# A two-block transformer step on one core: low halves of the weights by an accumulating DMA in place of a subtraction

## The chip, the cores and the metric

One core of a Trainium2 chip runs the whole program in one launch. The metric is the device time of one execution in microseconds (us).

## The reference

Two blocks work on 512 tokens of width 1024. The first block mixes with two kinds of attention (8 heads each of 64), attends to 256 memory rows (4 heads of 256) and has a gated FFN with a short convolution. The second block has a gating mixer over 128-token blocks, an MLP, a latent attention (8 heads) and a second MLP. Cut to its products:

```python
proj = rmsnorm(x) @ w_in                        # 1024 x 3080
x = x + concat(fox_attention, stick_breaking) @ w_out
x = x + softmax(q @ k.T / 16) @ v @ w_mo        # q from w_mq, k and v of the memory from w_mkv
u = causal_conv(rmsnorm(x) @ w_up)              # 1024 x 5632
x = x + (silu(gate) * val) @ w_down             # 2816 x 1024
h = h + (u * (W_s v + b)) @ a_w_out             # u, v = gelu(hn @ a_w_in)
h = h + square(relu(rmsnorm(h) @ w1)) @ w2      # 1024 x 4096 x 1024, twice
h = h + mla(hn) @ b_w_o
```

## The kernel before

Every fp32 product is made of three matmuls of a format with fewer bits: each operand is split into a high half (a cast to `F32R`) and a low half (what the cast lost), and `mm3` (L196) adds high by high, high by low and low by high. Activations are split once and stay. Weights are streamed: `weights` (L169) makes one unit of k rows of tiles by n columns, most often 128 partitions x 1024 numbers (512 KB), in these steps.

- SyncE loads the unit from HBM into `st`, tile `wst` (L176). The pool `p_wst` has 2 buffers (L118).
- ScalarE casts it to the high half, `wh` (L181). The pool `p_w` has 4 buffers for `wh` and 4 for `wl` (L119).
- VectorE or GpSimd subtracts: `wl = wst - wh` (L182). Which of them is named by a letter of `self.low`: "d" is VectorE, "p" is GpSimd. In the mixers the letters are taken from `LOW`, in the latent attention from `LATENT_LOW`; elsewhere all are "d".

A unit whose rows are scaled by gains (`gain`, 16 units for the latent projections) is made by `split` (L160) instead. With `apart` the very first unit goes in two halves.

The products are `tform` (L203: the weights are the stationary side, one unit is one chunk of 128 outputs), `tokens` (L212: the activations are stationary) and `down` and `last_down` (L274, L978: second products, unit by unit over the inner dimension, with the activation chunk split at L271 beside each unit). The stages run in order: `begin`, `mixers`, `memory`, `ffn`, `gmlp`, `mlp(0)`, `mla`, `mlp(1)` (L483 to L491). In the mixers and the latent attention, tables of due times (`FILL`, `LATENT_FILL` and others) weave the heads' work with units of later products. Then a scheduler orders the instructions of each engine by a simulated timeline; each engine takes its own in that order, one after the other.

GpSimd's other work is masks (L688), scaling of probabilities (L259), sums of squares (L349), additions at boundaries (L396), powers (L321), the FFN's gate product (L902) and the gating product (L1103). ScalarE's evacuations that the text speaks of are L954 (MLP, `square`) and L892 (FFN).

Of the kernel before, what the change touches and what calls it, by code (L numbers as in the profile page):

```python
# [12 lines left out]
F32 = mybir.dt.float32  # L13
# [4 lines left out]
ALU = mybir.AluOpType  # L18
# [42 lines left out]
def weave(*lanes):  # L61

    heap = [(times[0], i, 0) for i, (times, _) in enumerate(lanes)]
    heapq.heapify(heap)
    while heap:
        t, i, k = heapq.heappop(heap)
        times, gen = lanes[i]
        if next(gen, None) is not None:
            k += 1
            heapq.heappush(heap, (times[min(k, len(times) - 1)], i, k))  # L70


def even(t0, t1, n):
    return [t0 + (i + 0.5) * (t1 - t0) / n for i in range(n)]


def filling(gens, plan, t0):

    times, parts = [], []
    for i, (name, n, t1) in enumerate(plan):  # L80
        times += even(t0, t1, n)
        more = any(name == later[0] for later in plan[i + 1:])
        parts.append(itertools.islice(gens[name], n) if more else gens[name])
        t0 = t1
    return times, itertools.chain(*parts)


def run(gen):
    for _ in gen:
        pass  # L90
# [2 lines left out]
FILL = [['qk1', 16, 0.8], ['qk3', 16, 2.082], ['qk2', 12, 2.247], ['qk2', 4, 3.296], ['v', 32, 5.5], ['qk4', 16, 7.129], ['qk5', 16, 8.229], ['qk6', 10, 8.354], ['mk', 12, 8.992], ['qk6', 1, 9.307], ['mk', 8, 10.003], ['mk', 6, 10.525], ['qk6', 5, 10.752], ['mk', 8, 11.39], ['qk7', 16, 12.667], ['mv', 32, 15.302], ['out', 32, 16.79]]  # L93
FOX_SCALE = 'pppd'
LATENT_SCALE = 'dpad'
LOW = 'ppppppdppppp'
LATENT_LOW = 'ddpppppppppp'
NORM_FOX = 12.316
SCORES = [-0.68, 0.106]
MIX_OUT = 1.347  # L100
# [7 lines left out]
class Kernel:  # L108
# [60 lines left out]
    def weights(self, src, shape, gain=None, apart=False):  # L169

        k, n = shape
        low = next(self.low)
        st = self.p_wst.tile([P, k, n], F32, tag="wst", name="wst")
        parts = [slice(j, j + 1) for j in range(k)] if apart else [slice(0, k)]
        for j in parts:
            self.nc.sync.dma_start(st[:, j], src[:, j])  # L176
        h = self.p_w.tile([P, k, n], F32R, tag="wh", name="wh")
        l = self.p_w.tile([P, k, n], F32R, tag="wl", name="wl")
        if gain is None:
            for j in parts:  # L180
                self.nc.scalar.copy(h[:, j], st[:, j])  # L181
                self.engines[low].tensor_sub(l[:, j], st[:, j], h[:, j].bitcast(F32))  # L182
        else:
            for j, g in enumerate(gain):
                self.split(h[:, j], l[:, j], st[:, j], scale=g)
        return h, l
# [292 lines left out]
    def run(self):  # L479
        a, nc = self.a, self.nc  # L480
        self.steps, self.later, self.waiting, self.turn = 0, [], [], 6
        self.engines, self.low = {"d": nc.vector, "p": nc.gpsimd}, itertools.repeat("d")
        self.begin()  # L483
        self.mixers()
        self.memory()
        self.ffn()
        self.gmlp()
        self.rope_tables()
        self.mlp(0)
        self.mla()  # L490
        self.mlp(1)  # L491

    def begin(self):
# [16 lines left out]
        for b in range(NB):  # L510
            self.ingest(b, xs[b], g, xT, self.x)
            block = next(values)
            if b == 0:
                run(itertools.islice(block, 7))
            nc.vector.tensor_copy(col[:, b:b + 1], self.block_rstd(xs[b]))
            run(block)
# [197 lines left out]
    def mixers(self):  # L714
        a, nc = self.a, self.nc
        self.qk, self.rows = {}, {}
        cd = self.forget()
        self.sb_scale = self.scaled_cols(0.125)
        run(self.qk_pair(0))
        self.low = itertools.cycle(LOW)  # L720
        mixed = [self.s8([P, 4, T]) for _ in range(2)]
        accs = [self.t2("acc") for _ in range(2)]
        v_sb = []
        parts, fox_part = {}, []

        def stats(kind, bank):
            return self.spread(self.rstd_from(self.mean_sq(accs[kind], 512, bank=bank), NB), bank)

        def split_mixed(kind, row=None):

            parts[kind] = self.s8([P, 4, T], F32R), self.s8([P, 4, T], F32R)
            for pr in range(4):
                m = mixed[kind][:, pr]
                g = self.g[("fox", "sb")[kind]][:, pr:pr + 1]
                if row is not None:
                    nc.vector.scalar_tensor_tensor(m, m, g, row, op0=ALU.mult, op1=ALU.mult)
                self.split(*(t[:, pr] for t in parts[kind]), m, scale=g if row is None else None)

        def normed_fox():
            row = stats(0, "f")  # L740
            yield 1
            split_mixed(0, row)
            yield 1

        def fox_out():

            fox_part.extend(self.s8([P, 4, T]) for _ in range(2))

            def evac(m, ps):
                nc.scalar.copy(fox_part[m // 4][:, m % 4], ps)  # L750

            yield from self.down(lambda k: tuple(t[:, k] for t in parts[0]), a["w_out"][0, 0:512], 4, evac,
                                 [(range(3), range(4)), (range(3, 6), range(4)), (range(6, 8), range(4))], bank="f")

        def values_sb():
            v_sb.extend(self.s8([P, NB, 4, 2, 64], F32R) for _ in range(2))
            for block in self.vproj(v_sb, 2560):
                yield from block

        gens = {"mk": self.memory_keys(), "mv": self.memory_values(), "v": values_sb(), "out": fox_out()}  # L760
        gens.update({f"qk{pr}": self.qk_pair(pr) for pr in range(1, 8)})
        lanes = [filling(gens, FILL, -0.4), ([NORM_FOX, NORM_FOX + 0.3], normed_fox())]
        for hd in range(16):
            kind = hd // 8
            v = (self.v_fox, v_sb)[kind]
            head = self.fox_head(hd, cd) if kind == 0 else self.sb_head(hd - 8)
            lanes.append((even(hd + SCORES[0], hd + SCORES[1], 4), head))
            lanes.append(([hd + MIX_OUT + t for t in ATTEND], self.mix_head(hd, v, mixed[kind], accs[kind])))
        weave(*lanes)
        self.low = itertools.repeat("d")  # L770
        self.x = [self.s8([P, 4, T]) for _ in range(2)]
        for h in range(2):
            nc.scalar.dma_start(self.x[h].rearrange("p k t -> p (k t)"), self.x_dram[h])
        split_mixed(1)
        for m in range(8):
            nc.gpsimd.tensor_add(self.xc(m), self.xc(m), fox_part[m // 4][:, m % 4])
        out = self.down(lambda k: tuple(t[:, k] for t in parts[1]), a["w_out"][0, 512:1024], 4,
                        self.boundary(self.g["xattn"], rows=False, scale=lambda: row),
                        [(range(3), range(3)), (range(3, 7), range(3)), (range(3), [3]), (range(3, 7), [3]), ([7], range(4))], 1)
        run(itertools.islice(out, 21))  # L780
        row = stats(1, "o")
        run(out)
# [387 lines left out]
    def mla(self):  # L1170
        a, nc, n = self.a, self.nc, self.norm
# [53 lines left out]
        def values(pr):  # L1225

            u = self.w_rows(wkv, 0, 2, 512 * pr, 512)
            v = self.s8([P, NB, 2, 256], F32R)
            kv[pr] = u, v
            for b2 in range(2):  # L1230
                ps = self.ps("f")
                for b in range(2):
                    cols = slice((2 * b2 + b) * P, (2 * b2 + b + 1) * P)
                    out = ps[:, 256 * b:256 * b + 256].rearrange("p (h n) -> p h n", n=P)
                    for k in range(2):
                        xh, xl = ckv.at(k)
                        vw = tuple(t[:, k].rearrange("p (h n) -> p h n", n=256)[:, :, 128:256] for t in u)
                        self.mm3(out, (xh[:, cols], xl[:, cols]), vw, k == 0, k == 1)
                    yield 1
                s = slice(2 * b2, 2 * b2 + 2)  # L1240
                self.split(v[:, s, 0], v[:, s, 1], ps.rearrange("p (b n) -> p b n", b=2))
# [30 lines left out]

        self.low = itertools.cycle(LATENT_LOW)
        run(values(0))
# [85 lines left out]
            lanes.append((even(hd + LATENT_SCORES[0], hd + LATENT_SCORES[1], 4), scores(hd)))  # L1360
            lanes.append(([hd + LATENT_OUT + t for t in LATENT_ATTEND], outputs(hd)))
        weave(*lanes)
        self.low = itertools.repeat("d")
        run(out)


# [21 lines left out]
```

## Time and profile before

| | us |
|---|---|
| median of 2 runs | 2012.53 (2012.41 to 2012.64) |
| profiled execution | 2014.74 |
| its span, first to last instruction | 2013.0 |
| TensorE busy | 1962.5 |
| VectorE busy | 1149.5 |
| ScalarE busy | 881.7 |
| GpSimd busy | 385.4 |

Busy times come from one profiled execution; the span leaves out 1.7 us around the first and the last instruction. Matmuls overlap in their pipeline, so a full TensorE row means that one started as soon as the one before allowed it. DMA-issuing instructions are not counted as busy.

### The profile page before, as it was taken

The page shows a single profiled execution, that of the slowest core. Times are in us where ns is not written, and L with a number is a line of the kernel's source. Part 1 is how long each engine was busy: PE and PEld are TensorE (multiplying, and loading weights), DVE is VectorE, ACT ScalarE, POOL GpSimd, SP SyncE. Part 2 cuts the span into 40 slices and gives each one's busy share as a digit, 9 for nine tenths or more (in the row PEclk, how much of TensorE's full clock was granted, in tenths as well). Part 3 has the DMA queues.
Part 4 walks back from the last instruction along what each step waited for, and adds up shares of the span by engine and source line. Part 5 has one row for each costly group of instructions (what it writes and reads, how often), then busy time and mean ns, then how long its engine had stood idle before and what let it go on. Part 6 is the DMA issues. An engine that isn't in the chain of part 4 may idle for free.

```text
span 2013.0 us, 24501 instructions
## 1 busy us (share of the span) xinstructions
PE 1962.5 (97%) x9199; PEld 1633.6 (81%) x9199; DVE 1149.5 (57%) x1968; ACT 881.7 (44%) x1531; POOL 385.4 (19%) x316
## 2 busy tenths in 40 slices
PE   8998899999999999999999999999999999999998
PEld 7786777788888888888888888888898878888887
DVE  6778886547766533756875733333477774333334
ACT  6667564435443332545344432223356644322223
POOL 2675774202111100401220100000032320000000
PEclk9998999999999999999999999999999999999999
DMA  6322334213333322332223333232232123332232
GB/s 182 105 85 74 95 96 135 59 61 105 105 94 95 103 96 94 95 94 84 82 79 104 108 97 94 96 103 95 72 89 61 54 60 112 95 98 91 95 99 80
DMA packets 216391, 187.24 MB, mean 93 GB/s; under 512 B 12321, under 2 KB 189001, under 8 KB 215761
## 3 DMA queue, kind: packets, MB, share of 16 engines
q1 hardware_dynamic: 213953, 178.32, 29.7%
q10 hardware_dynamic: 2320, 7.36, 1.0%
q8 instruction: 72, 1.18, 0.2%
q14 instruction: 46, 0.38, 0.1%
HBM read 181.44 MB, written 4.21 MB: 92 GB/s over the span
## 4 chain that ended last, share of the span: by engine, by line
PE 81%; DVE 9%; ACT 3%; issue 3%; DMA 3%; POOL 2%; SPq 0%; POOLq 0%; ACTq 0%; DVEq 0%
PE ps_f L199 13%; PE ps_f L201 12%; PE ps_f L200 12%; PE ps_s L200 6%; PE ps_s L199 6%; PE ps_s L201 6%; PE ps_t L199 6%; PE ps_t L200 6%; PE ps_t L201 6%; PE ps_o L200 2%; PE ps_o L199 2%; PE ps_o L201 2%; DMA wst<-in_w_in 1%; DVE ex L690 1%; DVE wl L182 1%
## 5 line engine op out<-in xcount | busy, mean ns | idle before, releaser
L181 ACT CAST wh<-wst 128x1024 fp32r<-128x1024 f32 (+4 forms) x352 | 344.4, 979 | 648.8 <-PE ps_f L200 296.9
L182 DVE TENSOR_TENSOR wl<-wst,wh 128x1024 fp32r<-128x1024 f32 (+4 forms) x296 | 352.4, 1191 | 291.9 <-ACT wh L181 283.1
L201 PE MATMUL ps_f<-s,wl 128*128 128x512 f32 (+1 forms) x912 | 351.8, 387 | 3.8 <-DVE wl L182 3.8
L200 PE MATMUL ps_f<-s,wh 128*128 128x512 f32 (+1 forms) x912 | 352.6, 387 | 1.9 <-DVE s L167 1.8
L199 PE MATMUL ps_f<-s,wh 128*128 128x512 f32 (+1 forms) x912 | 349.2, 390 | 2.7 <-DVE f L805 1.5
L201 PEld LDWEIGHTS ps_f<-s,wl 128*128 128x128 f32 x912 | 173.1, 190 | 37.7 <-DVE wl L182 4.6
L199 PEld LDWEIGHTS ps_f<-s,wh 128*128 128x128 f32 x912 | 173.3, 190 | 36.0 <-DVE f L805 1.7
L200 PEld LDWEIGHTS ps_f<-s,wh 128*128 128x128 f32 x912 | 172.8, 190 | 34.2 <-DVE s L167 3.0
L349 POOL TENSOR_TENSOR acc<-acc,sq 128x512 f32<-128x512 f32 x46 | 75.5, 1648 | 633.8 <-ACT sq L348 632.9
L163 ACT CAST ch<-s 128x512 fp32r<-128x512 f32 (+1 forms) x166 | 77.5, 495 | 152.7 <-PE ps_s L200 100.2
L182 POOL TENSOR_TENSOR wl<-wst,wh 128x1024 fp32r<-128x1024 f32 (+3 forms) x56 | 123.7, 2212 | 98.6 <-ACT wh L181 98.6
L164 DVE TENSOR_TENSOR cl<-s,ch 128x512 fp32r<-128x512 f32 (+1 forms) x166 | 85.8, 535 | 87.5 <-ACT ch L163 87.5
L321 POOL TENSOR_TENSOR sm<-sm,m_half 128x1 f32<-128x1 f32 (+1 forms) x31 | 26.6, 859 | 495.1 <-DVE sm L338 351.9
L199 PE MATMUL ps_s<-s,wh 128*128 128x512 f32 x280 | 109.5, 392 | 0.4 <-ACT pp L849 0.4
L200 PE MATMUL ps_s<-s,wh 128*128 128x512 f32 x280 | 109.2, 390 | 0.0
L201 PE MATMUL ps_s<-s,wl 128*128 128x512 f32 x280 | 109.0, 390 | 0.0
L199 PE MATMUL ps_t<-s,wh 128*128 128x512 f32 x272 | 105.9, 390 | 0.0
L200 PE MATMUL ps_t<-s,wh 128*128 128x512 f32 x272 | 105.9, 389 | 0.0
L201 PE MATMUL ps_t<-s,wl 128*128 128x512 f32 x272 | 105.1, 389 | 0.0
L200 PE MATMUL ps_f<-cl,wh 128*128 128x512 f32 x210 | 82.1, 391 | 0.0
L199 PE MATMUL ps_f<-wh,s 128*128 128x512 f32 (+2 forms) x208 | 77.2, 376 | 4.8 <-ACT s L163 3.3
L201 PE MATMUL ps_f<-ch,wl 128*128 128x512 f32 x210 | 81.8, 389 | 0.0
(460 smaller groups left out, 4122.2 us busy)
## 6 DMA issues: line engine op xcount, KB each, us to landing
wst<-in_mlp_w SPq DMA_DIRECT2D x128, 512.0 KB
wst<-in_w_up SPq DMA_DIRECT2D x44, 512.0 KB
wst<-in_a_w_in SPq DMA_DIRECT2D x32, 512.0 KB
wst<-in_w_in SPq DMA_DIRECT2D x23, 512.0 KB
wst<-in_w_down SPq DMA_DIRECT2D x22, 512.0 KB
wst<-in_w_mkv SPq DMA_DIRECT2D x16, 512.0 KB
wst<-in_a_w_out SPq DMA_DIRECT2D x16, 320.0 KB
wst<-in_w_mq SPq DMA_DIRECT2D x8, 512.0 KB
```

What stands on the lines that cost most here:

```text
L163: nc.scalar.copy(hi, src)
L164: nc.vector.tensor_sub(lo, src, hi.bitcast(F32))
L181: self.nc.scalar.copy(h[:, j], st[:, j])
L182: self.engines[low].tensor_sub(l[:, j], st[:, j], h[:, j].bitcast(F32))
L199: mm(out, lhsT=ah, rhs=bh, start=first, stop=False)
L200: mm(out, lhsT=ah, rhs=bl, start=False, stop=False)
L201: mm(out, lhsT=al, rhs=bh, start=False, stop=last)
L321: self.nc.gpsimd.tensor_tensor(r, ms, self.m_half[:, 0:n], op=ALU.pow)
L349: (nc.vector if last else nc.gpsimd).tensor_add(acc, acc, sq)
L690: nc.vector.tensor_tensor_scan(ex[:, :n][:, ::-1], kp[:, :n][:, ::-1], self.ones[:, 0:1].to_broadcast([P, n]), 1.0, op0=ALU.mult, op1=ALU. ...
```

## The change

For units without gains and not `apart`, ScalarE makes the cast and then `wl = -wh`; a DMA issued by GpSimd adds the staged unit to `wl` in place, so that it becomes `wst - wh`. All letters become "m". The remaining subtractions (the two halves of the first unit) go to VectorE. The buffers of the pools stay as they are. Behind the insertion the lines move down by 4; in the new code the cast is L180, the negated copy L181, the accumulating DMA L182.

```diff
-LOW = 'ppppppdppppp'
-LATENT_LOW = 'ddpppppppppp'
+LOW = 'm'
+LATENT_LOW = 'm'
...
-        if gain is None:
+        if gain is None and not apart and low == "m":
+            self.nc.scalar.copy(h, st)
+            self.nc.scalar.mul(l, h.bitcast(F32), -1.0)
+            self.nc.gpsimd.dma_start(l, st, accum_op=ALU.add)
+        elif gain is None:
             for j in parts:
                 self.nc.scalar.copy(h[:, j], st[:, j])
-                self.engines[low].tensor_sub(l[:, j], st[:, j], h[:, j].bitcast(F32))
+                self.nc.vector.tensor_sub(l[:, j], st[:, j], h[:, j].bitcast(F32))
...
-        self.engines, self.low = {"d": nc.vector, "p": nc.gpsimd}, itertools.repeat("d")
+        self.engines, self.low = {"d": nc.vector, "p": nc.gpsimd}, itertools.repeat("m")
...
-        self.low = itertools.repeat("d")
+        self.low = itertools.repeat("m")
```

The last pair stands twice, behind the mixers and behind the latent attention. In numbers of instructions: ScalarE gets 350 more (`wl<-wh`), GpSimd 350 DMAs and 56 subtractions less, VectorE 294 subtractions less. The order of the instructions changes with it.

ScalarE in the first product of the first MLP, before: `wh` and `wst` are the unit's tiles, `f` the evacuated chunk and `s8` where its square goes.

```order
L181 CAST wh_10433<-wst_10431 128x1024
L954 ACTIVATE s8_9882<-f_10326 128x512
L181 CAST wh_10467<-wst_10465 128x1024
L954 ACTIVATE s8_9883<-f_10360 128x512
L181 CAST wh_10501<-wst_10499 128x1024
```

The same engine and place now:

```order
L180 CAST wh_10642<-wst_10640 128x1024
L958 ACTIVATE s8_10076<-f_10532 128x512
L181 ACTIVATE wl_10643<-wh_10642 128x1024
L180 CAST wh_10677<-wst_10675 128x1024
L958 ACTIVATE s8_10077<-f_10567 128x512
L181 ACTIVATE wl_10678<-wh_10677 128x1024
```

The negated copy of a unit stands behind an evacuation (of a chunk three units earlier) that follows the unit's cast. In the second products it stands right behind the cast.

GpSimd at the boundary behind the mixer's output product, before: `s_3573` and `s_3574` are the residual, `f` the scaled output, `acc` the sum of squares.

```order
L396 TENSOR_TENSOR s_3573<-f,s_3573 128x512 x4
L349 TENSOR_TENSOR acc<-acc,sq 128x512
L396 TENSOR_TENSOR s_3574<-f,s_3574 128x512
L349 TENSOR_TENSOR acc<-acc,sq 128x512
L396 TENSOR_TENSOR s_3574<-f,s_3574 128x512 x2
L349 TENSOR_TENSOR acc<-acc,sq 128x512
L396 TENSOR_TENSOR s_3574<-f,s_3574 128x512
L349 TENSOR_TENSOR acc<-acc,sq 128x512 x3
```

The same place now:

```order
L400 TENSOR_TENSOR s_3618<-f,s_3618 128x512 x2
L182 DMA wl<-wst 128x1024
L400 TENSOR_TENSOR s_3618<-f,s_3618 128x512 x2
L353 TENSOR_TENSOR acc<-acc,sq 128x512
L400 TENSOR_TENSOR s_3619<-f,s_3619 128x512 x2
L353 TENSOR_TENSOR acc<-acc,sq 128x512
L182 DMA wl<-wst 128x1024
L400 TENSOR_TENSOR s_3619<-f,s_3619 128x512 x2
L353 TENSOR_TENSOR acc<-acc,sq 128x512
L182 DMA wl<-wst 128x1024
L353 TENSOR_TENSOR acc<-acc,sq 128x512 x2
L182 DMA wl<-wst 128x1024
```

DMAs of the units of the next product stand among the additions, and each waits for its negated copy on ScalarE before GpSimd goes on.

## Rows read from the trace of the kernel before

**Rows 1.** The page's part 1: busy us, share of the span, instructions.

```profile
PE 1962.5 (97%) x9199; PEld 1633.6 (81%) x9199; DVE 1149.5 (57%) x1968; ACT 881.7 (44%) x1531; POOL 385.4 (19%) x316
```

**Rows 2.** Busy time by stage: attention, FFN up, gating output, MLP second product.

```profile
core 0: us, PE busy (x) PEld busy (x) DVE busy (x) ACT busy (x) POOL busy (x), PEclk, DMA share, GB/s
...
60.00:320.00 260.00, 238.22 (x1237) 198.29 (x1238) 205.16 (x433) 171.44 (x350) 174.09 (x155) 0.97 0.32 97
...
460.00:686.00 226.00, 225.72 (x999) 186.40 (x999) 151.94 (x181) 97.83 (x121) 35.21 (x26) 1.00 0.35 103
...
994.00:1097.00 103.00, 103.00 (x484) 85.83 (x483) 70.88 (x124) 45.71 (x85) 16.67 (x10) 1.00 0.29 85
...
1271.00:1441.00 170.00, 170.00 (x751) 140.81 (x750) 57.01 (x62) 49.27 (x63) 0.00 (x0) 1.00 0.29 96
```

**Rows 3.** Timeline of ScalarE, first MLP, first product: start us, us, instruction, idle before.

```profile
1179.45 1.06 ACT L181 CAST wh<-wst 128x1024 fp32r<-128x1024 f32 x1 [3.86 <-issue]
1180.41 0.62 ACT L954 ACTIVATE s<-f 128x512 f32<-128x512 f32 x1
1184.89 1.05 ACT L181 CAST wh<-wst 128x1024 fp32r<-128x1024 f32 x1 [3.86 <-PE ps_f L200]
```

**Rows 4.** Chain of waits from 330 to 342 us: start us, us, what.

```profile
332.85 0.69 DVE wl L182
333.54 0.02 issue
333.55 3.91 DMA wst<-in_w_mq
...
337.57 1.06 ACT wh L181
...
338.65 1.23 DVE wl L182
```

**Rows 5.** Waits of SyncE's DMA queue: us in total, times, longest us.

```profile
SPq L176 <- DVE wl L182: 1290.9, 267, 18.8
SPq L176 <- POOL wl L182: 288.3, 52, 24.4
```

**Rows 6.** Groups by shape: count, busy us, mean ns, idle before and its releasers.

```profile
L182 DVE TENSOR_TENSOR wl<-wst,wh 128x1024 fp32r<-128x1024 f32 x245 | 307.0, 1254 | 246.7 <-ACT wh L181 241.3 <-PE ps_o L201 4.4 <-PE ps_t L418 0.8
L181 ACT CAST wh<-wst 128x1024 fp32r<-128x1024 f32 x279 | 293.2, 1051 | 570.5 <-PE ps_f L200 276.4 <-issue 85.6 <-PE ps_t L200 58.0
...
L182 POOL TENSOR_TENSOR wl<-wst,wh 128x1024 fp32r<-128x1024 f32 x34 | 91.5, 2692 | 49.3 <-ACT wh L181 49.3
```

**Rows 7.** Chain of waits, other stretches: two DMAs and the first boundary.

```profile
57.67 2.51 DMA cdram<-kp
...
349.02 1.38 POOL acc L349
...
1465.73 2.92 DMA wst<-in_kv_w_a
```

**Rows 8.** Timelines of the gating output: ScalarE at 768 columns, VectorE at 640.

```profile
1041.92 0.84 ACT L181 CAST wh<-wst 128x768 fp32r<-128x768 f32 x1 [1.17 <-PE ps_f L200]
1046.00 0.73 ACT L181 CAST wh<-wst 128x640 fp32r<-128x640 f32 x1 [1.15 <-PE ps_f L200]
...
1096.40 0.83 DVE L182 TENSOR_TENSOR wl<-wst,wh 128x640 fp32r<-128x640 f32 x1 [1.97 <-ACT wh L181]
1099.80 0.83 DVE L182 TENSOR_TENSOR wl<-wst,wh 128x640 fp32r<-128x640 f32 x1 [1.97 <-ACT wh L181]
```

**Rows 9.** ScalarE's casts of line 181 in the attention stage: us, busy (count).

```profile
60.00:320.00 260.00, 38.91 (x40) 0.97 0.32 97
```

**Rows 10.** Timeline of GpSimd from 255 to 300 us.

```profile
262.21 8.23 POOL L182 TENSOR_TENSOR wl<-wst,wh 128x1024 fp32r<-128x1024 f32 x1 [3.04 <-ACT wh L181]
...
271.51 2.36 POOL L182 TENSOR_TENSOR wl<-wst,wh 128x1024 fp32r<-128x1024 f32 x1
```

More of the change, by code (lines that the diff above doesn't have):

```diff
@@ L1362, in mla @@
         weave(*lanes)
-        self.low = itertools.repeat("d")
+        self.low = itertools.repeat("m")
         run(out)
```

## The prediction

> **What bounds the kernel now.** I read the page's busy times first. TensorE is busy 97% of the span [rows 1]; the windows by stage then show where the other 3% are: 260 us of the head attention stage hold 238 us of matmuls, while the FFN, the gating output and the MLPs are full from edge to edge [rows 2]. Of all 50 us without a matmul, 22 are in that attention stage. Whatever the change takes off VectorE or GpSimd, it cannot gain more than these idle times. (A measurement of this kernel tells about 2%, 40 us, from no change.)
>
> So the question is how much slack the supply of weights has. The timeline of ScalarE in the first product of an MLP shows the casts of `wh` 5.44 us apart [rows 3]: that is one 128x1024 unit, 24 matmuls. The casts end their wait at a matmul (most of their idle time, 276.4 us, in [rows 6]): a cast waits for TensorE to give back one of the four `wh` buffers, so three units are always ready and a longer way to the low half does no harm by itself. What has fewer buffers is the staged unit: `wst` has two. Its cycle is seen in the chain of waits, in a stretch in which it lay open: the load is issued 0.01 us after the subtraction ends, lands 3.91 us later, the cast takes 1.06 us, the subtraction 1.23 us [rows 4]. That is about 6.3 us, against 10.88 us for two units, the time that TensorE gives to two buffers. SyncE's own waits say the same: 1290.9 us in 267 waits, 4.8 us each, for VectorE's subtraction to free a staged unit [rows 5]; the load itself is early.
>
> **The change part by part.** 350 units lose their subtraction: 294 of VectorE's 296 and all 56 of GpSimd's. A 128x1024 one costs VectorE 1254 ns, GpSimd 2692 ns [rows 6]. In the full stages this gives nothing, since VectorE is off the path there. Added are 350 multiplications on ScalarE, priced as its casts, 1.05 us at 128x1024 [rows 6], and 350 DMAs issued by GpSimd. ScalarE rises from 882 to some 1225 us of 2013, which alone binds nothing.
>
> The accumulating DMA keeps the staged unit: it can only be overwritten when the addition has read it, and SyncE's next load waits for the DMA's completion. Call the time from the end of the multiplication to that completion A. No GpSimd DMA and no accumulating one is in the trace, so A is bounded. From below: the shortest DMA of the chain, 16 KB, takes 2.51 us [rows 7], nearly all of it latency. From above: two complete loads one after the other, 2 x 3.91 = 7.82 us. In between: a load keeps the 16 DMA engines busy 0.29 x 5.44 = 1.58 us (share from rows 2, period from rows 3), so 3.91 us are 2.3 us latency and 1.6 us of data; an accumulate reads two units, the staged one and the negated copy, so 2.3 + 2 x 1.6 = 5.5 us. I take this: it has the load's row for both parts, and lies near the middle.
>
> Now the cycle of a `wst` buffer. In the first products (FFN 44 units, MLPs 64) the order puts an evacuation of 0.62 us [rows 3] between cast and multiplication: 3.91 + 0.11 + 1.05 + 0.62 + 1.05 + 0.04 + A = 6.78 + A, with the hops of rows 4. With A = 5.5 that is 12.28 us for two units instead of 10.88, so 0.70 us more per unit, x 108 = 76 us. Where only cast and multiplication stand (FFN down 22, MLP second products 64, gating values 16) it is 6.16 + A = 11.66, 0.39 us more, x 102 = 40 us. The gating output has smaller units, which TensorE eats faster: 3.40 us for 640 columns, 4.08 us for 768 [rows 8]. At 640 the load is 2.92 us [rows 7], A shrinks to 2.3 + 0.625 x 3.2 = 4.3: 2.92 + 0.11 + 2 x 0.73 + 0.04 + 4.3 = 8.83 against 6.80, 1.02 us x 16 = 16 us; at 768, by the same scaling, 10.0 against 8.16, 0.93 x 8 = 8 us.
>
> In the attention stage 40 units go through 260 us [rows 2, 9], 13 us for two: 11.66 fits, with 1.3 us left, which the waits in ScalarE's and GpSimd's in-order queues will use. GpSimd's queue is the one with an added wait. The DMA waits there for the multiplication, and behind it stand the scalings of probabilities, masks, and, at the boundary after the mixer, the additions that are on the path (row 349.02 in [rows 7]; three DMAs now stand among them). In exchange GpSimd is free of 2.7 us subtractions. I book +10 us for the attention stage (bounds: -22, its idle time, to +60, 1.5 us on each of 40 units), +5 us for boundaries, +10 us for the memory attention and the latent attention. The sum is 76 + 40 + 24 + 25 = 165 us. It is made against the profiled execution (2014.74 us, span 2013.0), which is 2 us above the median of 2012.53; on the median it gives 2178 us, 8% slower.
>
> A rule that speaks for less. The nearest row is the load from HBM, 3.91 us for 512 KB [rows 4]. The Trainium skill, "DMA: Bandwidth & Descriptors", section "Anatomy of one DMA — SWDGE (gpsimd) path", gives a GpSimd DMA about 2.0 us plus bytes over 436 GB/s: 3.2 us for a plain 512 KB copy. By it, if adding cost nothing, the stages of 108 and 102 units would lose nothing and the time would be near 2030 us; with a doubled data part, 4.4 us, it would be near 2060 us. The row stands above the rule already without an addition, so I stay with the row.
>
> **The rivals.** (a) The DMA fits into the slack, A at or below 4.1 us. For it: both sides are on the chip, and a load's 2.3 us of latency includes a trip to HBM. Then only the 640 and 768 units lose, some 0.5 us x 24, and the attention stage nothing: about 2030 us, not slower. It decides at A = 4.1, where 6.78 + A reaches 10.88. (b) As (a), and GpSimd's queue is freed where its subtractions were on the path: the most is the 22 us without a matmul in the attention stage, so about 1990 us; ScalarE's extra 1 us per unit speaks against.
>
> (c) GpSimd is held up by VectorE while it issues. One subtraction on GpSimd at 262.21 us took 8.23 us while VectorE ran, its neighbour 2.36 [rows 10]. If each DMA waits for one VectorE instruction, 1.25 us [rows 6], A = 6.7: +140 +101 +38 +45 = 324, so 2337 us. Against it: after the change VectorE is idle most of the time in the full stages (57.01 us busy of 170 already before [rows 2]). The Trainium skill, "SBUF — State Buffer", section "SBUF: two separate sides", states such a hold for the writing of descriptors beside VectorE instructions in a two-port mode; the slow GpSimd subtraction agrees that the two meet, though it is no DMA.
>
> (d) The DMA engines themselves become the bound: adding runs at a quarter of a load's rate, 6.3 us of all 16 engines, and with the load's 1.58 a unit needs 7.9 us. It decides from 5.44 - 1.58 = 3.9 us per accumulate. Then 2.46 x 210 = 517, plus some 40 for the small units and 80 for the attentions: about 2650 us. For it: nothing in the trace shows how fast a DMA adds; against it: the engines are busy for only 0.29 to 0.35 of these stages [rows 2]. (e) That the change does less than it says: three loads (two halves of the first unit, the forget columns) and 16 units with gains keep their old way; too few to matter.
>
> **How the numbers follow.** Forecast, A between 4.1 and 7: 0.48; (a) 0.22; (b) 0.05; (c) 0.12; (d) 0.13. The upper bound A = 7.82 gives 1.86 x 108 + 1.55 x 102 + 46 + 60 = 465 us, 2478 us. The range goes from 2015, which leaves out (b) and the better half of (a), to 2480, which leaves out (d) only. Slower by over 2%: the forecast almost whole, (c) and (d), 0.72; faster by over 2% needs nearly all of TensorE's idle time, 0.03; the rest, 0.25, is within 2%.
>
> **What would show it.** Right: in the FFN and the MLPs the casts stand about 6 us apart and end their wait at a DMA of `wst`, no longer at a matmul; TensorE falls to some 90% there and waits for `wl`; SyncE waits for the accumulate. VectorE falls by about 350 us, ScalarE rises by about 340. The attention stage keeps its length within some 20 us. Wrong: casts still 5.44 us apart, so A is under 4.1; or a DMA share near 1, so the engines bind and (d) holds; or the loss sits in the attention stage, behind GpSimd's queue, and not in the full stages.

## The result and the profile after

The changed kernel takes 2430.24 us (median of two runs, 2421.19 and 2439.30) against 2012.53: ratio 1.208, interval 1.188 to 1.227, so 418 us slower. 2178 us had been forecast, 165 us more. The direction was right and the time lies in the range, but the loss is two and a half times the one worked out.

The page of the changed kernel: busy times, DMA queues, two groups of the weight path, and the accumulating DMA (KB each, us from issue to landing).

```profile
span 2437.6 us, 25356 instructions
...
PE 2105.6 (86%) x9199; PEld 1683.9 (69%) x9199; DVE 763.9 (31%) x1674; ACT 1187.4 (49%) x1883; POOL 540.4 (22%) x610
...
q0 software_dynamic: 50400, 168.58, 37.9%
q1 hardware_dynamic: 213953, 178.32, 25.2%
...
DMA 57%; issue 15%; PE 12%; ACT 11%; DVE 3%; POOL 1%; POOLq 0%; ACTq 0%; SPq 0%; DVEq 0%
...
L180 ACT CAST wh<-wst 128x1024 fp32r<-128x1024 f32 (+4 forms) x350 | 341.7, 977 | 1080.8 <-DMA wst<-in_mlp_w 456.7
L182 POOL DMA_DIRECT2D wl<-wst x350 | 303.9, 869 | 1626.1 <-ACT wl L181 1442.1
...
wl<-wst POOLq DMA_DIRECT2D x279, 512.0 KB, 5.4
```

Against [rows 1], TensorE is busy 86% instead of 97% and has only 12% of the chain of waits; DMAs have 57%. Against [rows 6], the casts no longer wait for a matmul but for the load of `wst`. The accumulate lands 5.4 us after its issue (median), where A = 5.5 had been taken. Of GpSimd's 540.4 us, 303.9 are the issuing of these DMAs, which this page does count as busy.

Busy time of the changed kernel by stage (mixers, FFN up, gating output, MLP second product), the columns as in [rows 2]:

```profile
60.00:400.00 340.00, 279.45 (x1325) 226.94 (x1323) 174.39 (x444) 224.20 (x414) 122.88 (x169) 0.90 0.61 140
...
550.00:853.00 303.00, 256.62 (x1051) 201.94 (x1052) 94.29 (x134) 134.91 (x161) 68.98 (x67) 0.96 0.69 152
...
1228.00:1351.00 123.00, 105.74 (x457) 82.95 (x456) 49.62 (x87) 60.46 (x102) 33.19 (x33) 0.97 0.63 141
...
1560.00:1763.00 203.00, 188.37 (x781) 147.18 (x780) 21.47 (x31) 80.70 (x99) 28.71 (x34) 0.98 0.73 172
```

The DMA share is 0.61 to 0.73 where [rows 2] have 0.29 to 0.35: two thirds on the mean, not full. SyncE's waits, answering to [rows 5]:

```profile
SPq L176 <- DMA wl<-wst: 2164.6, 345, 28.0
```

Nearly every load now waits for an accumulate: the ring of two staged units is closed, as forecast. How long one turn of it takes is seen in the chain of waits in FFN up (start us, us, what):

```profile
640.39 3.94 DMA wst<-in_w_up
...
654.23 6.50 DMA wst<-in_w_up
...
660.80 3.01 issue
663.81 0.02 POOLq L182
663.83 4.54 DMA wl<-wst
668.36 0.02 SPq L176
668.38 0.03 issue
668.41 6.48 DMA wst<-in_w_up
...
674.96 3.01 issue
...
677.99 4.54 DMA wl<-wst
...
682.57 6.53 DMA wst<-in_w_up
```

The turn from load to load is 14.16 us (668.41 to 682.57); 12.28 had been forecast. The 3.01 us of "issue" are cast, evacuation and negated copy on ScalarE and the 0.3 us until GpSimd issues the DMA. ScalarE's timeline:

```profile
660.81 1.05 ACT L180 CAST wh<-wst 128x1024 fp32r<-128x1024 f32 x1 [7.45 <-DMA wst<-in_w_up]
661.76 0.81 ACT L896 ACTIVATE kp<-f,conv2b 128x512 f32<-128x512 f32 x1
662.48 1.04 ACT L181 ACTIVATE wl<-wh 128x1024 fp32r<-128x1024 f32 x1
...
664.78 1.03 ACT L180 CAST wh<-wst 128x1024 fp32r<-128x1024 f32 x1
...
674.97 1.05 ACT L180 CAST wh<-wst 128x1024 fp32r<-128x1024 f32 x1 [7.50 <-DMA wst<-in_w_up]
...
678.94 1.03 ACT L180 CAST wh<-wst 128x1024 fp32r<-128x1024 f32 x1
```

The casts come in pairs, 4.0 and 10.2 us apart, where [rows 3] have an even 5.44. The negated copy of the first buffer ends at 663.52 and its addition lands at 668.36, so A is 4.84 us for this buffer, less than forecast; for the second of the pair it is 5.87 us. The load that follows takes 6.48 us instead of 3.91: it runs while the other buffer (cast at 664.78) is being added. The load of 3.94 us at 640.39 was issued 0.66 us before the next addition (641.05 on GpSimd), the one of 6.48 us 0.64 us behind one (667.77).

Where the time went, by the first load of each weight on SyncE in the two traces:

| stage | before | after | lost | forecast |
|---|---|---|---|---|
| begin and mixers | 329.4 | 411.0 | 82 | 10 |
| FFN up, 44 units | 226.1 | 302.9 | 77 | 31 |
| FFN down, 22 | 119.7 | 144.8 | 25 | 9 |
| gating input, 32 | 189.2 | 230.1 | 41 | 6 |
| gating output, 24 | 102.8 | 123.1 | 20 | 24 |
| first MLP, 64 | 340.1 | 412.1 | 72 | 35 |
| memory and latent attention | 330.2 | 356.5 | 26 | 10 |
| second MLP, 64, to the end | 375.6 | 457.1 | 82 | 35 |

The forecasts are the prediction's terms, split by the units of each stage; its 5 us for boundaries stand in no row. The losses add up to the 425 us between the two profiled executions.

### The profile page after: what moved, and what is told of

Read it like the earlier page. It is cut to its first block, busy times and chain, and to the rows that moved or that the text cites. A ratio compares the mean times of both kernels' runs of the same rounds, so it can differ in the third digit from the quotient of the medians.

```text
span 2437.6 us, 25356 instructions
## 1 busy us (share of the span) xinstructions
PE 2105.6 (86%) x9199; PEld 1683.9 (69%) x9199; DVE 763.9 (31%) x1674; ACT 1187.4 (49%) x1883; POOL 540.4 (22%) x610
## 3 DMA queue, kind: packets, MB, share of 16 engines
q0 software_dynamic: 50400, 168.58, 37.9%
## 4 chain that ended last, share of the span: by engine, by line
DMA 57%; issue 15%; PE 12%; ACT 11%; DVE 3%; POOL 1%; POOLq 0%; ACTq 0%; SPq 0%; DVEq 0%
DMA wl<-wst 24%; DMA wst<-in_mlp_w 14%; DMA wst<-in_w_up 5%; ACT wl L181 3%; DMA wst<-in_w_down 3%; DMA wst<-in_a_w_in 3%; ACT wh L180 3%; PE ps_f L204 2%; PE ps_f L203 2%; PE ps_f L205 2%; DMA wst<-in_w_in 2%; DMA wst<-in_a_w_out 2%; ACT ch L163 1%; DMA wst<-in_w_mkv 1%; DMA wst<-in_w_out 1%
## 5 line engine op out<-in xcount | busy, mean ns | idle before, releaser
L180 ACT CAST wh<-wst 128x1024 fp32r<-128x1024 f32 (+4 forms) x350 | 341.7, 977 | 1080.8 <-DMA wst<-in_mlp_w 456.7
L182 POOL DMA_DIRECT2D wl<-wst x350 | 303.9, 869 | 1626.1 <-ACT wl L181 1442.1
L205 PE MATMUL ps_f<-s,wl 128*128 128x512 f32 (+1 forms) x912 | 365.3, 404 | 53.8 <-DMA wl<-wst 53.8
L203 PE MATMUL ps_f<-s,wh 128*128 128x512 f32 (+1 forms) x912 | 362.9, 401 | 26.9 <-ACT wh L180 14.0
L204 PE MATMUL ps_f<-s,wh 128*128 128x512 f32 (+1 forms) x912 | 361.1, 396 | 4.8 <-DVE s L167 4.8
L181 ACT ACTIVATE wl<-wh 128x1024 fp32r<-128x1024 f32 (+4 forms) x350 | 344.2, 984 | 4.0
L203 PEld LDWEIGHTS ps_f<-s,wh 128*128 128x128 f32 x912 | 179.1, 197 | 65.9 <-ACT wh L180 18.3
L204 PEld LDWEIGHTS ps_f<-s,wh 128*128 128x128 f32 x912 | 179.1, 196 | 39.5 <-DVE s L167 6.3
L203 PE MATMUL ps_t<-s,wh 128*128 128x512 f32 x272 | 111.3, 409 | 0.1
L204 PE MATMUL ps_t<-s,wh 128*128 128x512 f32 x272 | 109.9, 404 | 0.0
L204 PE MATMUL ps_f<-wl,s 128*128 128x512 f32 (+2 forms) x208 | 83.3, 401 | 18.9 <-DMA wl<-wst 18.7
L203 PE MATMUL ps_f<-ch,wh 128*128 128x512 f32 x210 | 80.3, 409 | 14.6 <-ACT ch L163 11.7
L205 PEld LDWEIGHTS ps_s<-s,wl 128*128 128x128 f32 x280 | 54.0, 194 | 47.4 <-DMA wl<-wst 36.4
L205 PEld LDWEIGHTS ps_t<-s,wl 128*128 128x128 f32 x272 | 53.6, 197 | 47.6 <-DMA wl<-wst 36.2
```

The lines of the kernel that those rows point to most:

```text
L180: self.nc.scalar.copy(h, st)
L181: self.nc.scalar.mul(l, h.bitcast(F32), -1.0)
L182: self.nc.gpsimd.dma_start(l, st, accum_op=ALU.add)
L203: mm(out, lhsT=ah, rhs=bh, start=first, stop=False)
L204: mm(out, lhsT=ah, rhs=bl, start=False, stop=False)
L205: mm(out, lhsT=al, rhs=bh, start=False, stop=last)
```

## The experiments

**Is it the ring?** Three runs open or close it. The first reads the addend once more from HBM, so that the accumulate no longer holds the staged unit:

```diff
-            self.nc.gpsimd.dma_start(l, st, accum_op=ALU.add)
+            self.nc.gpsimd.dma_start(l, src, accum_op=ALU.add)
```

> The accumulating DMA reads the weight unit from HBM once more instead of the staged unit, so that a wst buffer is free again after the cast on ScalarE; number of DMAs, ScalarE's and GpSimd's work stay. Ring theory (the two wst buffers are the bound: load, cast, negated copy, issue, accumulate, one after the other): the buffer's cycle falls from about 12 to about 6 us, TensorE is full again in the FFN and the MLPs, 2040 to 2100 us in all. Rival, DMA engines (load and accumulate crowd the same 16 engines): the bytes stay, so 2300 us or more. Rival, queues (ScalarE's and GpSimd's in-order queues hold the units up): unchanged queues, 2300 us or more.

2095.07 us, 1.040 (1.037 to 1.043). The page and ScalarE's waits of this run:

```profile
q0 software_dynamic: 204768, 168.58, 57.7%
...
wl<-in_w_up POOLq DMA_DIRECT2D x44, 512.0 KB, 6.4
```

```profile
ACT wh L180 <- PE ps_f L204: 313.4, 124, 10.4
```

The addition is slower (6.4 us) and takes more of the DMA engines (57.7% against 37.9%), yet 335 of 418 us are gone and the casts wait for a matmul again. So the ring costs them, not the length of the addition or the mean load of the engines.

The second leaves the DMA out (low halves are then the negated high halves):

```diff
-            self.nc.gpsimd.dma_start(l, st, accum_op=ALU.add)
```

> The accumulating DMA is left out, so the low halves are only the negated copies of the high halves; the cast and the multiplication on ScalarE stay. Ring and DMA-engine theories: within 20 us of the kernel before, 1995 to 2030 us, since nothing holds wst longer than the cast. Queue theory with ScalarE as its place: 2100 us or more.

1988.54 us, 0.988 (0.985 to 0.990), TensorE 98% busy, a little under the range expected. ScalarE's 350 extra copies cost nothing by themselves, and taking the subtractions from VectorE and GpSimd is worth 24 us. All of these lie ahead of the memory attention: its first load is at 303.7 us, 25.7 earlier than before.

The third closes the ring of the kernel before, with no DMA added:

```diff
-        self.p_wst = pool("wst", 2)
+        self.p_wst = pool("wst", 1)
```

> The kernel before (subtractions, no accumulating DMA) with one wst buffer instead of two. Ring theory, by the same sum as for the change: load 3.91 + cast 1.05 + subtraction 1.23 + hops 0.14 = 6.33 us per unit against the 5.44 us that TensorE takes, 0.89 x 210 = 187 us in the full stages, 20 + 11 in the gating output, 50 in the mixers: about 2280 us. Since no accumulate crowds the load, its own length should hold here and the sum come out within 60 us. Rival (the loss of the change is made by queues, not by the buffers): under 2100 us.

2333.45 us, 1.158 (1.154 to 1.161). Its chain of waits in FFN up:

```profile
616.69 3.87 DMA wst<-in_w_up
...
620.64 1.06 ACT wh L181
...
621.72 1.24 DVE wl L182
622.97 3.86 DMA wst<-in_w_up
```

6.28 us a turn, as the rows of the kernel before add up to (3.91 + 0.11 + 1.06 + 1.23 and hops). The whole time is 53 us over the sum that was expected. The way of reckoning a ring was sound; with nothing beside it a load is 3.9 us.

**Which units?** One run makes low halves by DMA everywhere but in the mixers and the latent attention, where the letters of before are back; the other only there.

```diff
-LOW = 'm'
-LATENT_LOW = 'm'
+LOW = 'ppppppdppppp'
+LATENT_LOW = 'ddpppppppppp'
...
-                self.nc.vector.tensor_sub(l[:, j], st[:, j], h[:, j].bitcast(F32))
+                self.engines.get(low, self.nc.vector).tensor_sub(l[:, j], st[:, j], h[:, j].bitcast(F32))
```

> The letters of the head stages (mixers and latent attention) are those of before, all other units keep the accumulating DMA. If stages add up: the loss of the mixers (82 us by the first issue of the memory attention's weights, 411.0 against 329.4) and of the latent attention (about 17 us) go, 2325 to 2345 us. If the loss were one thing that moves with the whole (clock, or a queue that stays late), it would stay over 2380 us.

2321.76 us, 1.153 (1.150 to 1.156), 3 us under the range for stages that add up.

```diff
-        self.engines, self.low = {"d": nc.vector, "p": nc.gpsimd}, itertools.repeat("m")
+        self.engines, self.low = {"d": nc.vector, "p": nc.gpsimd}, itertools.repeat("d")
...
-        self.low = itertools.repeat("m")
+        self.low = itertools.repeat("d")
```

> The accumulating DMA only in the mixers and the latent attention, all other units subtract on VectorE. If stages add up: 2012 + 82 + 17 = about 2110 us. If relief of GpSimd's queue were worth something there, less than 2080 us.

2068.78 us, 1.027 (1.024 to 1.030), not the 2110 us of stages that add up but the range named for a relief of GpSimd's queue, which this run does not show by itself. The streamed products carry 309 us and the heads 56; the missing 53 of 418 come only when both are changed, and why is not shown.

**What in the addition?** A copy in place of the addition keeps the ring but reads one operand less (the low halves are then the weights):

```diff
-            self.nc.gpsimd.dma_start(l, st, accum_op=ALU.add)
+            self.nc.gpsimd.dma_start(l, st)
```

> The DMA copies the staged unit over the negated copy instead of adding (the low halves are the weights themselves). If reading the second operand is what fills the accumulate (5.4 us to landing at 512 KB): landing falls to about 4 us, its share of the DMA engines from 38% to about 20%, and the time to 2150 to 2300 us. Rival, adding is free and the time is latency: landing stays over 5 us and the time over 2390 us.

2084.05 us, 1.034 (1.030 to 1.038).

```profile
q0 software_dynamic: 50400, 168.58, 23.9%
...
wl<-wst POOLq DMA_DIRECT2D x279, 512.0 KB, 3.6
```

The time lies under the 2150 to 2300 us expected. At 3.6 us the ring has slack again; adding instead of copying costs 1.8 us a DMA and 346 us in all, and whether the second operand's reading or the addition itself takes them, this run cannot tell. The prediction had weighed the Trainium skill, "DMA: Bandwidth & Descriptors", section "Anatomy of one DMA — SWDGE (gpsimd) path", by which a plain copy of this size would take an estimated 3.2 us: the measured median of 3.6 us is above it, the shortest of the 279 copies, 2.85 us, under it, and the median addition 2.2 us above it.

With the negated copy on VectorE, ScalarE's part of the turn shrinks and VectorE works while GpSimd issues:

```diff
-            self.nc.scalar.mul(l, h.bitcast(F32), -1.0)
+            self.nc.vector.tensor_scalar(l, h.bitcast(F32), -1.0, None, op0=ALU.mult)
```

> The negated copy is made by VectorE instead of ScalarE. Ring theory: the cycle loses only what VectorE is quicker, and ScalarE's queue no longer holds the copy behind evacuations, 0 to 0.5 us per unit, 2300 to 2430 us. Queue theory (ScalarE's in-order queue makes most of the loss): under 2250 us. Port theory (GpSimd is held up by VectorE while it issues): GpSimd's issue of the DMA, 0.87 us, grows to over 1.5 us and the time rises over 2450 us.

2328.97 us, 1.156 (1.147 to 1.165).

```profile
L182 POOL DMA_DIRECT2D wl<-wst x350 | 308.2, 882 | 1544.1 <-DVE wl L181 1177.9
```

101 us less than the changed kernel, with a turn of 13.4 us in FFN up (casts at 641.91 and 655.34 us). GpSimd's issue takes 882 ns on the mean against 869. In the changed kernel itself the 183 issues that run beside VectorE for over half of their time take 873 ns on the mean, the 135 beside none 864. So rival (c), by which each DMA waits for a VectorE instruction, is not what costs the time.

The mean hides a hold, though. Nine of this run's 350 issues end 0.08 to 0.09 us behind the negated copy of another unit on VectorE, and take 0.90 to 1.43 us. The longest of them, and the copy:

```profile
1328.01 1.43 POOL L182 DMA_DIRECT2D wl<-wst  x1 [8.20 <-DVE sr L164]
...
1328.66 0.69 DVE L181 TENSOR_SCALAR wl<-wh 128x1024 fp32r<-128x1024 f32 x1
```

That is some 3 us of GpSimd's time in the whole run. The Trainium skill, "SBUF — State Buffer", section "SBUF: two separate sides", which the prediction had named for (c), states such a hold of descriptor writing beside VectorE instructions in a two-port mode. These rows agree with the hold; no row shows the mode.

Both edits together, negation on VectorE and addend from HBM:

> The accumulate from HBM (no ring) and the negated copy on VectorE. With the ring gone ScalarE's queue is what can still be late in the mixers: 2040 to 2070 us. If what is left there, 82 us over the kernel before, is the DMA's landing (6.6 us) or GpSimd's queue, it stays at 2085 to 2100 us.

2090.42 us, 1.037 (1.034 to 1.040), as from_hbm alone. With the ring open, the negated copy on ScalarE no longer matters; the last 3.7% are not its. Whether they are the DMA's landing or GpSimd's queue stays open.

**Why do loads take 6.5 us?** One guess was the load's short packets (512 bytes in the first products) against the addition's long ones. So the 108 units of the first products are loaded in rows of 4 KB, in the changed kernel and in the one before.

```diff
+    def w_long(self, w, c):
+        h, l = self.w_rows(w, (c % 8) * P, 1, min(c // 8 * 1024, w.shape[1] - 1024), 1024)
+        return tuple(t[:, 0].rearrange("p (k n) -> p k n", k=8) for t in (h, l))
...
-                w, ps = self.w_cols(wu, ch * P), self.next_bank()
+                w, ps = self.w_long(wu, ch), self.next_bank()
...
-            w, ps = self.w_cols(w1, c * P), self.next_bank()
+            w, ps = self.w_long(w1, c), self.next_bank()
```

> The changed kernel, but the 108 units of the FFN up product and of the MLPs' first products are loaded from 128 rows of 4 KB (a wrong part of the weights) and not from 1024 rows of 512 B; bytes, instructions and order stay. Contention theory (a load in short packets is crowded by the accumulate on the same 16 engines, 6.5 us instead of 3.9 in the FFN, 4.6 where the rows are long): a load there takes about 4.6 us, the two buffers' cycle falls from about 14 to 12.5 us, about 0.8 us less on each of 108 units, 2330 to 2360 us. Rival, ScalarE's order (the evacuation between cast and negated copy makes the first products slow): nothing changes there, 2400 to 2440 us.

2405.37 us, 1.194 (1.185 to 1.202). FFN up takes 283.6 us instead of 302.9; loads on the chain fall to 3.89 us on the mean there, but accumulates rise to 5.66. The whole gain is 25 us against the changed kernel, whose own two runs lie 18 apart: the guess, which asked for 2330 to 2360 us, missed, and the time lies in the range named for no change.

> The same edit on the kernel before, as a control: its loads are early, so both theories expect 2005 to 2018 us.

2014.34 us, 0.999: no difference.

Then the crowding by itself. To the kernel before with one staging buffer, each unit adds an accumulate of the same size that holds no staging buffer and that nobody reads:

```diff
-        self.p_wst = pool("wst", 2)
+        self.p_wst = pool("wst", 1)
...
+                self.nc.gpsimd.dma_start(self.extra[:, 0:k * n].rearrange("p (k n) -> p k n", k=k), h.bitcast(F32), accum_op=ALU.add)
...
+        self.extra = c.tile([P, 1024], F32, name="extra")
+        nc.vector.memset(self.extra, 0.0)
```

> The kernel before with a single staging buffer (2333 us by itself, its loads 3.92 us on the chain of waits), to which each of the 350 units adds one accumulating DMA from GpSimd's queue of the cast unit into a scratch tile that nobody reads. The unit's own low half is made as before, so the accumulate holds no staging buffer; it only moves its bytes on the same DMA engines while the next unit is loaded. Theory that an accumulate beside a load stretches the load: loads on the chain rise from 3.9 us to 5 to 6.5 us, and with 350 units in a ring of one the time rises to 2500 to 2800 us. Rival, that the long loads of the changed kernel come from the order in which SyncE's queue and the two buffers fall, and not from the engines: loads stay at about 4 us and the time stays within 30 us of 2333.

2794.61 us, 1.386 (1.382 to 1.391), 461 us over the single buffer alone. The chain of waits in FFN up:

```profile
699.34 1.24 DVE wl L182
...
700.59 6.42 DMA wst<-in_w_up
...
707.11 1.05 ACT wh L181
...
708.19 1.24 DVE wl L182
...
709.44 6.39 DMA wst<-in_w_up
```

The same load, cast and subtraction as in one_buffer_before, and only the load has changed: 3.87 to 6.4 us. An addition on the same DMA engines stretches it by 2.5 us. That is the 6.5 us of the changed kernel.

How it does so is seen in the DMA queues of this stretch (packets, MB, share of 16 engines; q0 is GpSimd's, q1 SyncE's), first from the load's issue at 700.59 to 704 us, then from 704 us to its landing at 707.01:

```profile
q0 software_dynamic: 121, 0.50, 97.8%
...
q1 hardware_dynamic: 1040, 0.52, 58.6%
q0 software_dynamic: 23, 0.03, 9.7%
```

The addition, issued 1.0 us ahead of the load (699.60), takes nearly all of the 16 engines' time until then, and none of the load's 1040 packets moves. The load is not slowed; it waits for the addition's packets and then moves in 2 us. The two loads of the changed kernel above, 3.94 us ahead of an addition and 6.48 us behind one, fit this order.

> As crowd, with the 108 units of the first products loaded in rows of 4 KB instead of 512 bytes (another part of the weights is multiplied there). If the load is stretched because its many short packets take turns with the accumulate's long ones, the loads in the first products fall to 4 to 4.6 us and the time lies 100 to 200 us under crowd. If the engines merely share their bandwidth, packet length does not matter: loads as in crowd, time within 40 us of it.

> Control for crowd_long: a single staging buffer, rows of 4 KB in the first products, no extra DMA. If a load by itself costs the same with either packet length, the time is within 30 us of 2333 and the loads on the chain are 3.7 to 4 us.

2727.71 us (1.353, 1.349 to 1.358) with the addition and 2304.64 us (1.143, 1.140 to 1.147) without; one_long, like crowd_long, multiplies another part of the weights. One load on the chain in FFN up, crowd_long and one_long:

```profile
707.17 5.76 DMA wst<-in_w_up
```

```profile
714.36 3.51 DMA wst<-in_w_up
```

Long rows make a load 0.4 us shorter alone and 0.6 us shorter in the crowd; the stretch is 2.25 us where it was 2.5. In crowd_long, too, the load's first packet moves only 3.5 us after its issue, in one_long 1.0 us after. So a load waits with either packet length, and short packets are not what suffers. By the 67 us between crowd and crowd_long both expectations missed (100 to 200, or within 40), but the control's 29 us are part of it; the control's time came as expected (within 30), its load of 3.51 us did not (3.7 to 4).

**A version that beats both.** What no_dma gained is in the mixers, and from_hbm opens the ring. So the kernel before, with the new branch of `weights` reading the addend from HBM, and with only 10 units of the mixers made by the DMA:

```diff
-LOW = 'ppppppdppppp'
+LOW = 'ppmppmdppmpp'
...
+            self.nc.gpsimd.dma_start(l, src, accum_op=ALU.add)
```

> The kernel before, but in the mixers every third unit gets its low half from an accumulate out of HBM (negated copy on ScalarE) instead of a GpSimd subtraction. The kernel without the DMA was 24 us faster than before, nearly all by the end of the mixers (weights of the memory attention first loaded at 303.7 against 329.4 us). If a third of this relief stays: 2000 to 2008 us. If the DMA's wait in GpSimd's queue costs as much as a subtraction: 2010 to 2030 us.

2002.89 us, 0.994 (0.992 to 0.996): 13 us faster than before, a small gain, but clear of the interval. The first load of the memory attention comes at 315.4 instead of 329.4 us.

> The same with the negated copy on VectorE. If ScalarE's queue is the tight one in the mixers: up to 8 us less than the kernel with the copy on ScalarE. If VectorE is: up to 8 us more.

2014.07 us, 1.000 (0.998 to 1.001): with the negation on VectorE, which was busy for 205 of 260 us there already [rows 2], the gain is gone; 11 us more, where up to 8 had been named. A third staging buffer, which would loosen the ring in another way, was not tried.

## Why the prediction was right and wrong

- **The ring is the cause: right.** Casts wait for `wst`, SyncE for the accumulate, TensorE falls to 85% in FFN up; from_hbm, which only lets go of the staged unit, gives back 335 of 418 us.
- **A = 5.5: right.** From the end of the negated copy to the landing it is 4.84 and 5.87 us for the two buffers of the pair above, and 5.5 us on the median of all 350.
- **The range: kept by luck.** Its upper end was made with a longer addition, A = 7.82; the addition was as forecast, and another term grew.
- **The step that failed: the term 3.91 in the cycle "3.91 + 0.11 + 1.05 + 0.62 + 1.05 + 0.04 + A".** It was read off a stretch with no accumulate in flight [rows 4]. With two buffers in the ring, one is loaded while the other is added, and crowd shows what that does to a load issued behind the addition: 6.4 us. The turn became 14.16 us in first products, 1.64 us a unit instead of 0.70. In second products the chain of the changed kernel has the load at 4.5 us and a turn of 12.04 (11.66 forecast):

```profile
1609.40 4.55 DMA wl<-wst
...
1614.01 4.53 DMA wst<-in_mlp_w
...
1618.61 2.82 issue
...
1621.44 4.58 DMA wl<-wst
```

  The turn is not the same throughout: over whole products the casts are 6.8 to 6.9 us apart in first products (turns of 13.5 to 13.8 us) and 6.2 to 6.8 in second ones (12.3 to 13.5). By the table the FFN and the MLPs lost 256 us where 110 had been forecast: 146 of the 260 us that are missing between the profiled executions.
- **A term left out.** Only 16 of the 32 units of the gating input were in the sum; the stage lost 41 us, not 6.
- **The mixers at +10: wrong.** They lost 82 us with `begin`, whose units stand in no term. In streams_only, where only 11 DMAs are issued ahead of the memory attention's first load, that load still comes 31 us late; in heads_only 42 us. The slack of 1.3 us on a turn was reckoned with the same 3.91 us. In this stage's chain of the changed kernel the DMAs fall on each other too:

```profile
179.85 7.39 DMA wl<-wst
...
187.29 6.65 DMA wst<-in_w_mkv
```

  14 us for these two alone, more than the 13 us that TensorE gives to a turn. The gain that was booked as rival (b) is real (no_dma is 25.7 us earlier at the end of this stage), and it is lost under the ring.
- **Rivals.** (a) asked for A at or below 4.1; only a plain copy, 3.6 us from issue, comes under it. (c) fell: issues beside VectorE take as long as others, but for the nine of neg_dve. (d) fell in its form: it asked for 3.9 us of all engines an accumulate, while 0.379 of 2437.6 us over 350 is 2.6. But its resource was the right one: a mean share of 0.7 is no bound, yet the two DMAs that share a ring are those that meet, and the later one waits. The prediction used the engines' share only to ask whether they fill up, never to ask what they do to the load's latency.
- **Signs named ahead.** VectorE falls by 386 us (350 named), ScalarE rises by 306 (340). The casts are 6.2 to 6.9 us apart on the mean (6 named), in much of these stages in pairs, which nothing in the prediction foresaw. The attention stage was to keep its length within 20 us and did not.

## What to carry to other kernels

A DMA in place of a compute step inside a ring of few buffers adds its whole latency to the ring, and to a load issued behind it the time that its packets hold the engines: sum the turn with durations taken while the other transfers run, not from a quiet stretch. Ask first what the new step holds, and whether the same bytes can come from somewhere that nobody waits for: here a slower, heavier DMA from HBM was 335 us better. A relief that is worth something in one stage should be bought in that stage alone; ten units in the mixers, added from HBM, gave 13 us where 350 units cost 418.

## What was not expected of the hardware

- An addition by DMA of 512 KB, both operands on the chip, takes 5.4 us from issue to landing on the median (the shortest 4.5) and 37.9% of the engines' time over the run; the plain copy 3.6 us (2.85) and 23.9%. From HBM the addition takes 6.4 to 6.7 us in FFN up, the gating input and the MLPs, and 57.7%, in 204768 packets instead of 50400.
- Issued 1 us behind an addition, a load of 512 KB takes 2.2 to 2.5 us longer with either packet length: none of its packets moves until the addition's are nearly through, though the engines' mean share in that stretch of crowd is 0.60.
- The issue of an adding DMA keeps GpSimd busy for 0.87 us on the mean, that of a copy for 0.55 us. A negated copy on VectorE that falls into the issue holds it to the copy's end (neg_dve, nine times).
- TensorE's busy time rose from 1962.5 to 2105.6 us with the same 9199 matmuls, at a granted clock of 0.949 on the mean instead of 0.993, 0.90 in the mixers, where it is busy 279 of 340 us. With 12% of the chain on TensorE, at most a small part of the loss can be this; it was not tested by itself.
